# A hybrid streaming encoder on one core: another order of the mixer's streams (key rotation two steps behind the query's, projection steps between the score pairs and around the first small products)

## The chip, the cores and the metric

The kernel runs on one core of a Trainium2 chip, as one launch. The metric is the time of the whole program on the device in microseconds (us). Engines: TensorE (PE, with its weight loads PEld), VectorE (DVE), ScalarE (ACT), GpSimd (POOL) and SyncE (SP), which issues the transfers. Each engine takes its instructions in the order in which the program lists them.

## The reference

The input x is 256 rows of 1024 in float32. There are two layers, and each adds three sub-layers to x, every one between two RMSNorms: half a SwiGLU (1024 to 2816 to 1024), a token mixer, and half a second SwiGLU.

```
x += 0.5 * post1(SwiGLU_1(pre1(x)))
x += postm(W_out [GDN | DiffAttn | SSD | mLSTM](split(W_in premix(x))))
x += 0.5 * post2(SwiGLU_2(pre2(x)))
```

The mixer projects x with W_in and hands the columns to four groups of 256 columns and four heads each. A is the gated DeltaNet: a causal convolution over four rows, SiLU, l2-normalised q and k, per-head decay, and a triangular solve in chunks of 64 rows. B is differential attention: q and k rotated (rotary), two softmax maps per head, the second weighted by a scalar and taken off the first, block-causal by chunks of 64. C is an SSD (Mamba-2) with a convolution, and D an mLSTM with exponential gates and a running maximum. Their outputs, normalised, are multiplied with W_out.

## The kernel before, in words

Everything is float32, and products are made from three parts: both operands are split into a high part and the rest, and the high by high, rest by high and high by rest products are summed. The weights come from memory by SP into six raw half buffers of 128 by 1024; `split_hi` copies the high part on ACT (L177) and `split_lo` subtracts it on DVE (L328, `lo_...`). Matrix products are issued by `mm` (L203). Small helpers issue most operations, so that their lines recur: L149 `act`, L177 `acopy`, L183 `tt` and its kin, L193 and L194 `ts`, L197 `stt`.

The program is written in the order in which it is to run, with no scheduler behind it. For the feed-forward layers the order is fixed by loops. The mixer's order comes from the string `ORDER` (L40 and L41): the mixer is written as eleven Python generators, one letter each, and `interleave` (L44) takes one step of the stream that a letter names. A stream that waits for another one's result yields nothing, its letter is left in the plan, and the next letters are tried until one can step. What the blocked stream issues on its way to the wait is already in the program by then. Both layers use the same string, so each effect appears twice, 570 us apart.

The streams: `p` the projections (one step is a quarter of a 256-column projection, 12 products), `w` the weight splits, `s` the small per-head quantities (decays, their cumulative sums), `g` the gated DeltaNet, `c` the SSD, `m` the mLSTM's gates, `d` the mLSTM, `r` the attention's rotation (first the query `bq`, then the key `bk`), `x` and `y` the two pairs of attention heads, `b` the attention's end.

```
        streams = dict(s=smalls(), g=gdn(), c=ssd(), m=mlstm_gates(), r=diff(), x=diff_pair(0), y=diff_pair(1), b=diff_end(),
                       d=mlstm(), p=projections(), w=splits())
        interleave(streams, ORDER)
```

The first small products: `projections` projects the DeltaNet's keys and queries (`ps_ak`, `ps_aq`), and `ev_conv` evaluates the convolution of each, two copies with a scale on ACT (`gqk<-ps_aq`) and six multiply-adds on DVE. `smalls` makes the decay matrices (`ps_D` on PE, `eD` and `ex` exponentials on ACT, `am` on DVE); then SiLU and squares (`gqk`, `gsq`) follow on ACT, behind a table load. `mlstm_gates` begins with a transpose of `am` (`ps_am`, L889), and `gdn` with the sums of the squares (`ps_ss`, two columns) and the 64 by 64 products of keys with keys and queries (`ps_gr`). `ps_av` is the projection of the DeltaNet's values.

The attention: `diff` rotates bq and bk (a product `ps_rot`, a multiplication on DVE `rot`, one on POOL, an addition on DVE, L1392 and the lines about it). `diff_unit` has ten steps for a pair of heads, five for the second 128 rows with 256 keys (steps 1 to 5) and five for the first 128 rows with 128 keys (steps 6 to 10). Steps 1 and 2 make the scores of one map each (`ps_sc`), mask them with a memset (L1400), take the maximum (L1404, `bmx`), exponentiate on ACT (`bpe`) and take the reciprocal of the sum (L1408, `bri`). Step 3 scales and subtracts the maps on DVE, step 4 transposes the result (`ps_pT`, L1421) and copies it on ACT (`bpe<-ps_pT`), and step 5 multiplies with the values (`ps_bo`, copied by ACT to `bo`). `mlstm` makes its decay matrix (`ps_r`, then two operations `dar` on DVE and an exponential), transposes the keys `dk` (`ps_dkt`), multiplies q with k (`ps_dqk`), adds up the states (`ps_kv`, `dC`) and reads them out (`ps_di`, `ps_dq`). `lo_wo` are splits of W_out, `wo` its products. PSUM tiles come from three pools with 2, 3 and 3 buffers; `ps_sc`, `ps_pT`, `ps_bo`, `ps_dqk` and their kin share one of them.

Of the kernel before, what the change touches and what calls it, by code (L numbers as in the profile page):

```python
# [36 lines left out]
LEVELS = (1, 2, 4, 8, 16, 32)  # L37
LOG1P = (1.9999999998039973, 0.6666667925329377, 0.3999869481212616, 0.2862062340096714, 0.2139426743705339,
         0.24409403382106099)
ORDER = ("wpspwmpwpwpppsppwppswggpppgppggpwwggpwpggppwdggpgwpwcpggpcgmpggcccgggggcmgggxmxcgggxgpwwppggpggcpggw"  # L40
         "pgwgpwgwgyppwwwwwppcprgppwcwwpwywwpwdyrpxppxpyxdxxpyppxypypyppdypyxpddpbdpbdpppwppwdp")  # L41


def interleave(streams, order):  # L44

    plan = list(order)

    def step(c):
        try:
            return next(streams[c]) is not None  # L50
        except StopIteration:
            del streams[c]
            return False

    def pick():
        for n, c in enumerate(plan):
            if c in streams and c not in plan[:n] and step(c):
                return plan.pop(n)
        return next((c for c in list(streams) if step(c)), None)

    while streams:
        assert pick() or not streams, "no stream can go on"
# [59 lines left out]
def hybrid_encoder(ctx: ExitStack, tc: tile.TileContext, t_in: dict, cst_d, out_d, layers=(0, 1), stages=("f1", "mix", "f2")):  # L122
# [675 lines left out]
    def mixer(l, nxt):  # L798
# [155 lines left out]
        def splits():  # L954
            last = 2 * ids[l, "wo", WO_ORDER[3]] + 1
            for n in range(2 * ids[l, "ak"] + 2, last + 1):
                while len(parts) <= n:
                    if room.get(n, "w") == "w":
                        k = ring.index(n) - 4
                        free = k < 0 or ring[k] in used  # L960
                    else:
                        free = "ext" in ready
                    if not free:
                        yield None
                        continue
                    split_to(n)
                    yield 0.0, 1.3
# [488 lines left out]
        def mlstm():  # L1456
# [75 lines left out]
            for t in range(2):  # L1532
# [20 lines left out]
                       d=mlstm(), p=projections(), w=splits())  # L1553
        interleave(streams, ORDER)
        return accs, finish
# [63 lines left out]
```

## Time and profile before

| | |
|---|---|
| three runs | 1166.54, 1167.22, 1170.3 us; median 1167.22 |
| the profiled execution | 1166.11 us |
| its span | 1164.3 us |
| first mixer | about 205 to 403 us |
| second mixer | about 776 to 974 us |

The profile is one execution. Times of rows are microseconds from the start of its span. A row of the timeline gives the start, the busy time, the engine, the line and the operation with its output and input, and in square brackets how long the engine had been idle before and what released it. A row of the chain of waits gives the start, the length, the engine and the tile. The slices by window give for each stretch the busy time and count of each engine and at the end the clock that TensorE was granted (1.00 is full), the busy share of the transfer engines and what they moved in GB/s.

### The profile page before, as it was taken

The page shows a single profiled execution, that of the slowest core. Times are in us where ns is not written, and L with a number is a line of the kernel's source. Part 1 is how long each engine was busy: PE and PEld are TensorE (multiplying, and loading weights), DVE is VectorE, ACT ScalarE, POOL GpSimd, SP SyncE. Part 2 cuts the span into 40 slices and gives each one's busy share as a digit, 9 for nine tenths or more (in the row PEclk, how much of TensorE's full clock was granted, in tenths as well). Part 3 has the DMA queues.
Part 4 walks back from the last instruction along what each step waited for, and adds up shares of the span by engine and source line. Part 5 has one row for each costly group of instructions (what it writes and reads, how often), then busy time and mean ns, then how long its engine had stood idle before and what let it go on. Part 6 is the DMA issues. An engine that isn't in the chain of part 4 may idle for free.

```text
span 1164.3 us, 20842 instructions
## 1 busy us (share of the span) xinstructions
PE 1111.1 (95%) x8484; PEld 1031.8 (89%) x8484; DVE 742.7 (64%) x1319; ACT 569.1 (49%) x953; POOL 43.9 (4%) x64
## 2 busy tenths in 40 slices
PE   7999999899979899999999999999998898999997
PEld 5999898899968799999899999978997777999996
DVE  6745646868777865545766555477878687744552
ACT  6634545534344654543655444364434446543442
POOL 0000000010201000000000000001112010000000
PEclk9999999989989999999999999998999898999999
DMA  8856555412325466556556655634224254756630
GB/s 264 311 199 217 162 177 172 127 55 73 110 73 181 145 220 215 173 190 218 195 167 218 212 173 179 199 88 130 81 67 131 76 164 157 222 182 212 212 115 36
DMA packets 148708, 189.12 MB, mean 162 GB/s; under 512 B 12175, under 2 KB 133251, under 8 KB 148484
## 3 DMA queue, kind: packets, MB, share of 16 engines
q1 hardware_dynamic: 148612, 187.79, 50.0%
q8 instruction: 66, 1.08, 0.4%
q14 instruction: 30, 0.25, 0.1%
HBM read 186.72 MB, written 1.05 MB: 161 GB/s over the span
## 4 chain that ended last, share of the span: by engine, by line
PE 80%; DVE 11%; ACT 4%; issue 3%; POOL 1%; DMA 0%; DVEq 0%; SPq 0%; ACTq 0%; POOLq 0%
PE pgu L203 41%; PE acc L203 20%; PE wo L203 3%; PE ps_dq L203 2%; PE ps_av L203 1%; DVE gQ L183 1%; PE ps_dv L203 1%; PE ps_aq L203 1%; PE ps_ak L203 1%; PE ps_sc L203 1%; PE ps_bq L203 1%; PE ps_xT L500 1%; DVE ny L183 1%; PE ps_do L203 1%; PE ps_gr L203 1%
## 5 line engine op out<-in xcount | busy, mean ns | idle before, releaser
L149 ACT ACTIVATE sg<-pgu 128x256 f32<-128x256 f32 x88 | 33.5, 384 | 267.9 <-PE pgu L203 267.7
L203 PE MATMUL pgu<-xhi,hi_g 128*128 128x256 f32 x592 | 164.0, 277 | 0.0
L203 PE MATMUL pgu<-xhi,hi_u 128*128 128x256 f32 x592 | 163.9, 277 | 0.0
L203 PE MATMUL pgu<-xlo,hi_g 128*128 128x256 f32 x592 | 163.8, 277 | 0.0
L203 PE MATMUL pgu<-xhi,lo_g 128*128 128x256 f32 x592 | 163.6, 276 | 0.0
L203 PE MATMUL pgu<-xhi,lo_u 128*128 128x256 f32 x592 | 163.6, 276 | 0.0
L203 PE MATMUL pgu<-xlo,hi_u 128*128 128x256 f32 x592 | 163.6, 276 | 0.0
L183 DVE TENSOR_TENSOR hf<-pgu,sg 128x256 f32<-128x256 f32 x74 | 31.4, 425 | 197.4 <-ACT sg L149 197.3
L203 PE MATMUL acc<-hi_d,mlo 128*128 128x512 f32 x352 | 138.6, 394 | 0.0
L203 PE MATMUL acc<-lo_d,mhi 128*128 128x512 f32 x352 | 138.0, 392 | 0.0
L203 PE MATMUL acc<-hi_d,mhi 128*128 128x512 f32 x352 | 137.1, 389 | 0.0
L328 DVE TENSOR_TENSOR lo_g<-raw_g,hi_g 128x1024 fp32r<-128x1024 f32 x88 | 104.1, 1220 | 18.3 <-ACT hi_g L177 18.3
L328 DVE TENSOR_TENSOR lo_d<-raw_d,hi_d 128x1024 fp32r<-128x1024 f32 x88 | 103.1, 1222 | 18.3 <-ACT hi_d L177 18.3
L203 PEld LDWEIGHTS pgu<-xlo,hi_g 128*128 128x128 f32 x592 | 111.3, 188 | 1.4
L203 PEld LDWEIGHTS pgu<-xhi,hi_g 128*128 128x128 f32 x592 | 111.2, 188 | 1.3
L203 PEld LDWEIGHTS pgu<-xhi,hi_u 128*128 128x128 f32 x592 | 111.2, 188 | 0.0
L203 PEld LDWEIGHTS pgu<-xhi,lo_g 128*128 128x128 f32 x592 | 111.2, 188 | 0.0
L203 PEld LDWEIGHTS pgu<-xlo,hi_u 128*128 128x128 f32 x592 | 111.1, 188 | 0.0
L203 PEld LDWEIGHTS pgu<-xhi,lo_u 128*128 128x128 f32 x592 | 111.1, 188 | 0.0
L328 DVE TENSOR_TENSOR lo_u<-raw_u,hi_u 128x1024 fp32r<-128x1024 f32 x88 | 104.2, 1219 | 8.1 <-ACT hi_u L177 8.0
L177 ACT ACTIVATE hi_g<-raw_g 128x1024 fp32r<-128x1024 f32 x88 | 88.4, 1048 | 8.4 <-PE pgu L203 7.8
L177 ACT ACTIVATE hi_u<-raw_u 128x1024 fp32r<-128x1024 f32 x88 | 88.9, 1047 | 1.7 <-DMA raw_u<-in_ffn_w_up 0.9
(497 smaller groups left out, 2515.7 us busy)
## 6 DMA issues: line engine op xcount, KB each, us to landing
raw_g<-in_ffn_w_gate SPq DMA_DIRECT2D x88, 512.0 KB
raw_u<-in_ffn_w_up SPq DMA_DIRECT2D x88, 512.0 KB
raw_d<-in_ffn_w_down SPq DMA_DIRECT2D x88, 512.0 KB
raw_wo<-in_w_out SPq DMA_DIRECT2D x16, 512.0 KB
raw_s<-in_w_in SPq DMA_DIRECT2D x4, 528.0 KB
g_ffn_post_g<-in_ffn_post_g SPq DMA_DIRECT2D x4, 512.0 KB
raw_cz<-in_w_in SPq DMA_DIRECT2D x4, 512.0 KB
raw_ak<-in_w_in SPq DMA_DIRECT2D x4, 512.0 KB
```

The lines of the kernel that those rows point to most:

```text
L149: return nc.scalar.activation(out=out, in_=in_, func=func, **kw)
L177: return nc.scalar.activation(out=out, in_=in_, func=AF.Copy, **kw)
L183: return (eng or V).tensor_tensor(out=out, in0=a, in1=b, op=op)
L203: return nc.tensor.matmul(out, lhsT=lhsT, rhs=rhs, start=start, stop=stop)
L328: V.tensor_sub(out=lo, in0=raws[n][:, 0:w * k2], in1=hi.bitcast(F32))
L500: nc.tensor.transpose(p[:, 128 * q:128 * q + 128], self.y[:, 512 * h + 128 * q:512 * h + 128 * q + 128], ident)
```

## The change

Only the two lines of `ORDER` differ.

```
-ORDER = ("wpspwmpwpwpppsppwppswggpppgppggpwwggpwpggppwdggpgwpwcpggpcgmpggcccgggggcmgggxmxcgggxgpwwppggpggcpggw"
-         "pgwgpwgwgyppwwwwwppcprgppwcwwpwywwpwdyrpxppxpyxdxxpyppxypypyppdypyxpddpbdpbdpppwppwdp")
+ORDER = ("wpspwpwpwpppsppwspmpwgpgppgppggpwwggpwpggppwggpgwpwcpggpcgmpggcccgggggcmgggcggggpwwppggpmdggcpggwpgw"
+         "gpwgwgpppwpwcprgprpwcpwxxpyypwdxpywpxpyxdxxpypwpxypypypwpwdypwwyxxpddpbdpbdpppwppwdp")
```

In steps: the mLSTM's first step comes behind half of the projection `av`; a further quarter of `av` stands between the sums of the squares and the `gr` products; the five small gate operations of the mLSTM come later, behind copies of the DeltaNet; the key's rotation follows the query's after two projection steps, where it stood behind the mLSTM's decay matrix; the first score steps of the two head pairs stand close to each other, with projection steps between, and the mLSTM's decay matrix behind them; the last steps of the pair `x` (scaling of the first 128 rows, transposes, values) come later. The number of steps of each stream is the same, and so are the orders of POOL and SP.

On ACT, ahead of the first small products, the two scaled copies of the query change places with the exponentials of `smalls`:

```order
 L177 ACTIVATE gqk<-ps_ak,vcol 128x256 x2
 L177 ACTIVATE hi_cx<-raw_cx 128x1024
-L177 ACTIVATE gqk<-ps_aq,vcol 128x256 x2
 L149 ACTIVATE eD<-ps_D 128x512 x2
 L149 ACTIVATE ex<-cum 128x96
+L177 ACTIVATE gqk<-ps_aq,vcol 128x256 x2
 L149 ACT_TABLE_LOAD
 L149 ACTIVATE gqk<-gqk 128x512
```

The copies stand directly ahead of the table load now, with both exponentials in front of them.

On DVE, between the rotation of the query and the first scores, before:

```order
L183 TENSOR_TENSOR bq<-bq,rot 128x512
L197 SCALAR_TENSOR_TENSOR mlo<-ps_mo,vcol,mhi 128x256 x2
L328 TENSOR_TENSOR lo_dq<-raw_dq,hi_dq 128x1024
L197 SCALAR_TENSOR_TENSOR mlo<-ps_mo,vcol,mhi 128x256 x2
L328 TENSOR_TENSOR lo_dq<-raw_dq,hi_dq 128x1024
L183 TENSOR_TENSOR dar<-ps_r,am 128x512
L183 TENSOR_TENSOR dar<-dar,cst 128x512
L183 TENSOR_TENSOR rot<-ps_rot,cst 128x512
L183 TENSOR_TENSOR bk<-bk,rot 128x512
L1400 MEMSET ps_sc 64x2x64
```

And the same place in the changed kernel:

```order
L183 TENSOR_TENSOR bq<-bq,rot 128x512
L197 SCALAR_TENSOR_TENSOR mlo<-ps_mo,vcol,mhi 128x256 x2
L183 TENSOR_TENSOR rot<-ps_rot,cst 128x512
L183 TENSOR_TENSOR bk<-bk,rot 128x512
L328 TENSOR_TENSOR lo_dq<-raw_dq,hi_dq 128x1024
L197 SCALAR_TENSOR_TENSOR mlo<-ps_mo,vcol,mhi 128x256 x2
L328 TENSOR_TENSOR lo_dq<-raw_dq,hi_dq 128x1024
L1400 MEMSET ps_sc 64x2x64
```

The key's two operations moved ahead of both splits, and the two `dar` operations out of this piece: they follow now behind four score steps (memset, maximum, reciprocal, twice for each head pair), ahead of the scaling of either pair, where two score steps and their scaling alternated before.

On ACT, at the end of the attention:

```order
 L177 ACTIVATE vaug<-ps_dv 128x4x64 x2
 L177 ACTIVATE hi_wo<-raw_wo 128x1024 x2
-L177 ACTIVATE bo<-ps_bo 128x2x64 x2
+L177 ACTIVATE bo<-ps_bo 128x2x64
+L177 ACTIVATE bpe<-ps_pT 128x256
+L177 ACTIVATE bo<-ps_bo 128x2x64
 L149 ACTIVATE bor_y<-bss,lnf 128x8
 L149 ACTIVATE bor_y<-bor_y,lnf 128x8
```

One more copy of transposed probabilities stands behind the two splits of W_out here, between the last two copies of the attention's output.

More of the change, by code (lines that the diff above doesn't have):

```diff
@@ L39 @@
          0.24409403382106099)
-ORDER = ("wpspwmpwpwpppsppwppswggpppgppggpwwggpwpggppwdggpgwpwcpggpcgmpggcccgggggcmgggxmxcgggxgpwwppggpggcpggw"
-         "pgwgpwgwgyppwwwwwppcprgppwcwwpwywwpwdyrpxppxpyxdxxpyppxypypyppdypyxpddpbdpbdpppwppwdp")
+ORDER = ("wpspwpwpwpppsppwspmpwgpgppgppggpwwggpwpggppwggpgwpwcpggpcgmpggcccgggggcmgggcggggpwwppggpmdggcpggwpgw"
+         "gpwgwgpppwpwcprgprpwcpwxxpyypwdxpywpxpyxdxxpypwpwxypypypwpwdypwwyxxpddpbdpbdpppwppwdp")
 def interleave(streams, order):
```

## The prediction

> **What bounds the kernel now.** I read the page first (span, busy shares), then the waits of TensorE in the stretch of one mixer, then the stretch cut into slices of 3.41 us with the clock granted in each, and last the chain of waits and the timelines of ScalarE and VectorE at the two places that the change touches. From the page:
>
> ```profile
> PE 1111.1 (95%) x8484; PEld 1031.8 (89%) x8484; DVE 742.7 (64%) x1319; ACT 569.1 (49%) x953; POOL 43.9 (4%) x64
> ```
>
> PE is busy 95% of the span, so a change of order can give back at most the twentieth in which it stands still, and what it does more slowly than it could. The profiled execution took 1166.1 us (its span, 1164.3, and 1.8 us around it) and lies 1.1 us under the median of the three times, 1167.2. The sum below starts from 1166.1. A difference of 0.3% is 3.5 us, about the least that a measurement of this kernel tells from no change.
>
> PE's waits between 205 and 403 us, the first layer's mixer (line waited at, engine and line waited for, us in total, times, longest):
>
> ```profile
> PE ps_sc L203 <- DVE bk L183: 3.3, 1, 3.3
> PE ps_am L889 <- DVE am L183: 2.5, 1, 2.5
> PE ps_sc L203 <- ACT bpe L149: 2.3, 1, 2.3
> ```
>
> The first is the wait for the rotated keys before the first attention scores, the second the wait ahead of the first small product, the third one between two units of scores. The second layer repeats the program 570 us later, so each term counts twice. The norms, the feed-forward layers, SP's queue of transfers and POOL's queue keep their order, so those are nothing in the sum.
>
> **Term A, around the first small products.** The slices there (PE busy, PEld, DVE, ACT, POOL, then the granted clock, DMA share, GB/s):
>
> ```profile
> 232.17:235.59 3.42, 2.60 (x23) 2.63 (x24) 1.42 (x4) 3.35 (x6) 1.22 (x5) 1.00 0.16 55
> 235.59:239.00 3.41, 3.41 (x55) 3.39 (x54) 2.33 (x6) 0.44 (x1) 0.00 (x0) 0.99 0.14 26
> 239.00:242.41 3.41, 3.41 (x41) 3.29 (x38) 1.77 (x5) 0.00 (x0) 0.00 (x0) 0.50 0.40 133
> 242.41:245.83 3.42, 3.42 (x18) 3.42 (x18) 2.14 (x7) 0.00 (x0) 1.62 (x2) 0.51 0.00 0
> 245.83:249.24 3.41, 3.41 (x32) 3.41 (x32) 2.02 (x6) 0.84 (x2) 1.14 (x1) 1.00 0.00 0
> ```
>
> For two slices, 6.8 us, the clock is half, and half of that, 3.4 us, is lost. It falls right behind a slice in which PE was never idle, so idle time alone didn't do it. What PE did in that slice stands in the chain of waits (start, us, engine, tile):
>
> ```profile
> 233.26 2.75 PE ps_av L203 x24
> 236.00 1.68 PE ps_ss L203 x16
> 237.68 3.52 PE ps_gr L203 x64
> 241.21 5.11 PE ps_av L203 x24
> ```
>
> The same 24 projection products of `av` take 2.75 us before and 5.11 us behind, and between them run the sums `ss` (two columns wide) and the 64 by 64 products `gr`. My reading is that a slice full of small products counts as little work and halves the clock of the next. Now the change. The multiplication `am` goes ahead of six vector operations on DVE, and half of `av` goes ahead of `ps_am`: the wait of 2.5 us there goes. What is late next is `ss`, which needs ScalarE's squares `gsq`. ScalarE's rows (start, us, line, operation):
>
> ```profile
> 228.81 0.84 ACT L177 ACTIVATE gqk<-ps_aq,vcol 128x256 f32<-128x256 f32 x2 [0.42 <-PE ps_aq L203]
> ...
> 231.31 1.28 ACT L149 ACT_TABLE_LOAD   x1
> ...
> 234.45 0.63 ACT L149 ACTIVATE gsq<-gqk 128x512 f32<-128x512 f32 x1
> ```
>
> The copy `gqk` from `ps_aq` now stands behind the two exponentials and directly ahead of the table load, so the load starts 0.8 us later and the last `gsq` ends near 235.9 in place of 235.08. PE, which no longer waits at `am`, has half of `av` done by about 233.3 (2.75 us from 230.5, where it went idle before) and then waits 2.5 us for `gsq`: it starts `ss` at 235.9, against 236.0 before. The idle time is thus moved and not removed, which is nothing in the sum, and what is left of the term is the clock. `gr` now stands behind 12 further `av` products, 1.4 us after `ss`. The slice 232.17 to 235.59 would hold 1.1 us of PE work, the next `ss` and most of an `av` quarter, the third nearly all of `gr`. Ends: if no slice is poor enough, the 3.4 us come back (A = -3.4); with one slice at half, A = -1.7; with two again, A = 0; with three A = +1.7, and with four A = +3.4, since the first slice with its idle time could halve the clock for `ss`, `av` and `gr` alike. I take 0, the row with two slices, because `gr`, `ss` and the idle time are all still there, in the same three slices.
>
> **Term B, the score pairs and what follows.** The slices there, in the same columns:
>
> ```profile
> 331.16:334.57 3.41, 1.03 (x12) 0.78 (x12) 2.13 (x3) 0.63 (x1) 0.29 (x1) 0.99 0.48 157
> 334.57:337.99 3.42, 1.16 (x5) 0.83 (x3) 2.00 (x6) 1.02 (x4) 0.00 (x0) 0.50 0.00 0
> 337.99:341.40 3.41, 3.41 (x14) 2.75 (x13) 2.10 (x8) 1.02 (x4) 0.00 (x0) 0.50 0.00 0
> 341.40:344.81 3.41, 3.41 (x18) 3.41 (x18) 2.11 (x7) 1.02 (x4) 0.00 (x0) 0.51 0.02 5
> 344.81:348.23 3.42, 3.34 (x29) 3.15 (x29) 2.17 (x8) 3.22 (x7) 0.00 (x0) 1.00 0.00 0
> ```
>
> A slice with PE busy 1.03 of 3.41 us is followed by half clock, and two full slices pass before the clock is whole again. VectorE in the same stretch, from the timeline:
>
> ```profile
> 327.08 1.22 DVE L328 TENSOR_TENSOR lo_dq<-raw_dq,hi_dq 128x1024 fp32r<-128x1024 f32 x1
> 328.21 0.87 DVE L197 SCALAR_TENSOR_TENSOR mlo<-ps_mo,vcol,mhi 128x256 fp32r<-128x256 f32 x2
> 329.00 1.21 DVE L328 TENSOR_TENSOR lo_dq<-raw_dq,hi_dq 128x1024 fp32r<-128x1024 f32 x1
> 330.13 0.68 DVE L183 TENSOR_TENSOR dar<-ps_r,am 128x512 f32<-128x512 f32 x1
> 330.85 1.15 DVE L183 TENSOR_TENSOR dar<-dar,cst 128x512 f32<-128x512 f32 x1
> 331.92 0.68 DVE L183 TENSOR_TENSOR rot<-ps_rot,cst 128x512 f32<-128x512 f32 x1
> 332.70 0.69 DVE L183 TENSOR_TENSOR bk<-bk,rot 128x512 f32<-128x512 f32 x1
> 334.73 0.17 DVE L1400 MEMSET ps_sc<- 64x128 f32 x1 [1.34 <-PE ps_sc L203]
> ...
> 339.73 0.35 DVE L193 TENSOR_SCALAR bpe<-bpe,bri 128x256 f32<-128x256 f32 x1
> ...
> 341.40 0.17 DVE L1400 MEMSET ps_sc<- 64x128 f32 x1
> ```
>
> Each softmax unit is a chain that starts with a memset of the masked corner: a pair of them takes 5.0 us (334.73 to 339.73), and the scaling of the pair 1.7 (to 341.40). The change puts `rot` and `bk` of the key ahead of two weight splits, so that the scores are there when DVE comes to them, and moves the two `dar` operations (1.8 us) behind the chains. DVE reached the end of `bk` at 333.4; without `dar` it is through with all that stands ahead of the chains at 331.6. So the first chain starts 3.1 us earlier. But four chains now follow each other (2 x 5.0 = 10.0, to 341.6), then `dar` (1.8, to 343.4), then the scaling of the first pair (1.7, to 345.1), 3.7 us later than before. The keys are there at 333.4 less the 1.8 and less the two splits and the small `mlo` pair that now come behind them (3.3, the rows at 327.08 to 329.00), at 328.3. From then PE has two pairs of scores (1.03 us for 12 products in the slice at 331.16, 2.1 for both) and the projection `dk`, 48 products (5.5, by the 2.75 for 24 of `av`): an estimated 7.6 us, so that it is through near 336. It then stands idle for over 8 us, where it waited 5.6 in two pieces before (3.3 and 2.3). The second pair's scaling, behind one weight split (1.2, a split of `lo_dq`'s size) and 1.7 of its own, ends near 348.0.
>
> What PE does from there, in the chain of waits:
>
> ```profile
> 346.58 1.10 PE ps_bo L203 x8
> 347.68 1.44 PE ps_dq L203 x12
> ...
> 364.18 0.96 PE ps_dqk L203 x30
> ```
>
> From 347.68 to 364.18 PE ran 16.5 us without a wait, at full clock. Changed, the first `dq` product (1.44) falls ahead of the wait for the second pair, and the small product `ps_bo` (1.10) comes behind it; about 15.9 remain behind 348.1, and `ps_dqk` would start at 364.0, 0.2 us earlier than before. That is the gain of the early keys: nearly nothing, since the order of DVE, and not the keys, decides when the second pair is ready. The clock stands against it. Two whole slices (337.99 to 344.81) are idle or nearly so; the clock is half when PE resumes at 345.1, and by the rows above is whole again two slices later, at 351.64. Of 6.5 us at half clock 3.25 are lost, of which 1.0 lies in the wait that PE would have had ahead of the second pair: 2.2 net. `ps_dqk` then starts 2.0 us later than before. In the old order the slow slices cost nothing of this kind, because DVE's chains bounded that stretch.
>
> Then the tail of the attention: the last unit's transposes now wait for the scores' products on DVE (behind `lo_wo` splits), and their copy on ScalarE stands behind this row:
>
> ```profile
> 366.42 2.01 ACT L177 ACTIVATE hi_wo<-raw_wo 128x1024 fp32r<-128x1024 f32 x2
> ```
>
> The last `ps_bo` waits for that copy, and the output projection, `ps_kv` and the mLSTM's state wait behind it on PE. Bounds: nothing, if the splits come early, and 2.0, the row. I take 1.5, since splits of `wo` stand right ahead of the copy and an engine takes its queue in order. B = 2.0 + 1.5 = 3.5. Its ends are -0.2 (whole clock, tail covered) and 5.2 (one more slice at half, 1.7).
>
> A rule of the Trainium skill, the page "TensorE: Matmul & The Clock Gate", section "HAM oscillation — how this bites in real kernels", says in the abstract that there should be no idle gap of PE over about 3.4 us. By it B's gap of 8 us halves the clock, as the row at 331.16 has it; A's gap of 2.5 us would not, and the sum would be by the rule 1166.3 where it is 1173.1 by the rows. The trace speaks against it as a full account, since the clock fell at 239.00 behind a slice with no idle time.
>
> **The sum.** 2 x (0 + 3.5) = +7.0: 1166.1 + 7.0 = 1173.1 us. With B from 2.0 to 5.2 this case spans 1170.1 to 1176.5.
>
> **Rivals.** *Faster*: the clock holds at the small products (A = -3.4), because `av` pieces on both sides of `ss` and ahead of `gr` keep each slice above the fall, and the tail's copies find cover (B between -0.2 and 2.0). For it: 2.60 us of work in the slice at 232.17 didn't halve the clock, so the fall lies below that. Against it: the same slice will hold 1.1 us, close to the 1.03 that did. It gives 2 x (-3.6) to 2 x (-1.4): 1158.9 to 1163.3, the middle 1161.1. It decides where no slice between 232 and 246 is granted half.
>
> *No change*: a gain at the small products and the loss behind the pairs cancel: A = -3.4 with B = 3.5 gives 1166.3, A = -1.7 with B = 2.0 gives 1166.7. For it: `gr` leaves the slice in which `ss` runs, which is the one sure difference there. Against it: it asks for two sizes to match.
>
> *Worse than forecast*: the idle time ahead of `ss` halves the clock at once, and `ss`, `av` and `gr` all run at half: A = +1.7 to +3.4, with B = 3.5 to 5.2: 1176.5 to 1183.3. For it: 1.1 of 3.42 us busy. Against it: that slice starts and ends with wide products.
>
> That the change doesn't do what it says is excluded for the keys: on DVE `bk` moves ahead of both splits, and no other stream holds it back.
>
> **How the numbers follow.** Chances: forecast 0.38, faster 0.22, no change 0.25, worse 0.15. The time is that of the likeliest, 1173.1. For 8 in 10 the range runs from 1162 (about half of the faster case, 0.12, is left out) to 1179 (half of the worse case, 0.07). Faster by over 0.3%: 0.22. Within it: 0.25 and the lower edge of the forecast, together 0.26. Slower: the rest, 0.52.
>
> **What would show it.** Right: no wait at `ps_am`, one of about 2.5 us at `ps_ss` for ScalarE; two slices at half clock near 239 to 246; the first score memset near 331.7 and the first pair's scaling not before 345; a wait of PE of 7 us or more at `ps_pT`, half clock from before 345 to near 351; a new wait at the last `ps_bo` for ScalarE's copy. Wrong: full clock through 232 to 246 (the faster case); a wait at `ps_pT` under 4 us, or full clock behind it, which would take 2 us out of B; no wait at `ps_bo`, which takes 1.5.

## The result, and the profile after

The changed kernel takes 1177.01 us (median of 6 runs, 1173.02 to 1178.12) against 1166.88 us (median of 6, 1164.34 to 1170.3). The ratio is 1.0066, 95% interval 1.0042 to 1.0090, so it is slower by 4.9 to 10.5 us, 7.7 by the ratio itself; the medians differ by 10.1. The forecast was 1173.1.

The profiled execution of the changed kernel took 1178.1 us, near the top of its runs, and that of before 1166.1. The two traces thus differ by 12.0 us, some 2 us more than the medians do.

```profile
span 1176.3 us, 20842 instructions
## 1 busy us (share of the span) xinstructions
PE 1124.1 (96%) x8484; PEld 1040.4 (88%) x8484; DVE 742.6 (63%) x1319; ACT 569.0 (48%) x953; POOL 44.9 (4%) x64
```

The same 8484 products keep PE busy for 1124.1 us, 13.0 more than before: PE doesn't wait longer in sum, its work takes longer. Where that happens is read off marks that both traces have (the start of a tile, in us):

| start of | first mixer: before | after | later by | second mixer: before | after | later by |
|---|---|---|---|---|---|---|
| `ps_D` | 228.61 | 228.93 | 0.3 | 798.80 | 806.97 | 8.2 |
| `ps_kt` (behind the small products) | 247.50 | 251.11 | 3.6 | 817.75 | 826.07 | 8.3 |
| first `ps_sc` of the SSD | 285.43 | 289.01 | 3.6 | 855.67 | 864.85 | 9.2 |
| last `cy` (end of the SSD) | 324.28 | 328.78 | 4.5 | 894.45 | 904.65 | 10.2 |
| `ps_dqk` | 364.11 | 367.27 | 3.2 | 934.44 | 944.09 | 9.7 |
| `ps_kv` | 369.11 | 375.33 | 6.2 | 939.44 | 952.13 | 12.7 |
| first `pgu` of the next feed-forward | 401.58 | 408.88 | 7.3 | 973.35 | 985.70 | 12.4 |

Four stretches have a price: the small products 3.3 us in the first layer and 0.15 in the second; the end of the SSD 0.9 and 1.0; the score pairs a gain of 1.3 and 0.55; the tail behind `ps_dqk` 3.1 and 3.0. The rest, 2.8 of the 12.4 us, lies outside these four: 0.3 ahead of the first mark, 0.9 in the feed-forward between the mixers, 0.9 ahead of the SSD in the second layer, and behind `ps_kv` 1.1 in the first layer less 0.3 in the second. PE's waits in the first mixer, 205 to 408 us:

```profile
PE ps_ss L203 <- ACT gsq L149: 2.5, 1, 2.5
PE ps_pT L1421 <- DVE bpe L197: 1.4, 5, 0.4
PE ps_sc L203 <- DVE bk L183: 1.3, 1, 1.3
...
PE ps_bo L203 <- ACT bpe L177: 0.7, 1, 0.7
PE ps_pT L1421 <- DVE dar L183: 0.5, 1, 0.5
```

The wait for `am` is gone and one of 2.5 us for `gsq` stands in its place. The keys are waited for 1.3 us where it was 3.3. The waits for the last `ps_bo` and for `dar` are new.

**The small products, first layer.** Slices of 3.41 us; the third number from the end is the granted clock:

```profile
233.72:237.13 3.41, 0.95 (x9) 0.95 (x9) 1.76 (x7) 3.29 (x5) 0.08 (x1) 1.00 0.00 0
237.13:240.55 3.42, 3.42 (x17) 3.42 (x18) 2.51 (x6) 0.00 (x0) 0.00 (x0) 0.50 0.30 63
240.55:243.96 3.41, 3.41 (x42) 3.19 (x41) 0.00 (x0) 0.00 (x0) 0.00 (x0) 0.50 0.27 95
243.96:247.37 3.41, 3.41 (x40) 3.29 (x37) 1.59 (x4) 0.00 (x0) 0.00 (x0) 0.50 0.00 0
247.37:250.79 3.42, 3.42 (x18) 3.42 (x18) 3.00 (x10) 0.84 (x2) 1.64 (x2) 0.50 0.00 0
```

Behind the idle slice (0.95 of 3.41 us busy) the clock is half, and it stays at half for four slices, in which `ss`, `av` and `gr` all run. The chain of waits shows what that does to each:

```profile
236.18 2.74 PE ps_ss L203 x16
238.92 2.77 PE ps_av L203 x12
241.69 4.45 PE ps_gr L203 x64
```

The sums take 2.74 us where they took 1.68, 12 products of `av` take 2.77 where 24 took 2.75, and `gr` takes 4.45 where it took 3.52. In the second layer the same rows lie otherwise:

```profile
810.61:814.03 3.42, 1.13 (x10) 0.93 (x8) 2.88 (x9) 3.35 (x5) 1.19 (x5) 0.99 0.16 54
814.03:817.44 3.41, 3.22 (x15) 3.22 (x16) 1.23 (x1) 1.09 (x2) 0.00 (x0) 0.50 0.00 0
817.44:820.85 3.41, 3.41 (x17) 3.19 (x18) 1.31 (x5) 0.00 (x0) 0.00 (x0) 0.51 0.53 153
820.85:824.27 3.42, 3.42 (x73) 3.35 (x72) 1.32 (x4) 0.00 (x0) 0.00 (x0) 1.00 0.01 2
```

Here the clock is whole again at 820.85, just as `gr` starts (820.49), and as far as `ps_kt` the price is that of before, two slices. The border of a slice fell a little otherwise against the same work. But `ps_kt` follows `gr` by 5.6 us there, by 9.5 in the first layer, and PE comes up against VectorE's chain that starts with the result of `gr`:

```profile
830.50 1.13 PE L203 MATMUL ps_y<-gQ,npbd 128*128 128x128 f32 x8 [0.20 <-DVE gQ L183]
```

The second group of `ps_y` waits as long, and both are through 6.9 us behind the start of `ps_kt` where it was 6.0 in the first layer. That is the 0.9 us ahead of the SSD, so that the part costs 1.0 us in the second layer and not 0.15.

**The end of the SSD.** VectorE's rows, and then POOL's at the same time:

```profile
327.41 0.16 DVE L183 TENSOR_TENSOR crr_a<-crr_a,crr_v 128x4 f32<-128x4 f32 x1
327.61 1.07 DVE L197 SCALAR_TENSOR_TENSOR ccr<-crr_a,crr_y 128x4 f32<-128x4 f32 x1
```

```profile
327.57 1.09 POOL L183 TENSOR_TENSOR bk<-bk,cst 128x512 f32<-128x512 f32 x1 [1.42 <-PE ps_rot L203]
```

An operation on four columns takes 1.07 us in place of 0.16: it ends when POOL's multiplication of the key ends. Before, POOL came to the key at 330.35, when `ccr` was long done. It held another operation up there, the second `dar`, whose row the prediction shows with 1.15 us. With POOL idle beside it the same operation takes 0.69. POOL in the kernel before, then `dar` in the changed one:

```profile
330.35 1.10 POOL L183 TENSOR_TENSOR bk<-bk,cst 128x512 f32<-128x512 f32 x1 [7.79 <-PE ps_rot L203]
```

```profile
347.24 0.69 DVE L183 TENSOR_TENSOR dar<-dar,cst 128x512 f32<-128x512 f32 x1
```

The change thus moved a hold of 0.46 us to a place where it costs 0.91.

**The score pairs.** VectorE's first memset of the scores and the two weight splits that follow the scalings of the two pairs:

```profile
336.13 0.17 DVE L1400 MEMSET ps_sc<- 64x128 f32 x1
...
349.58 1.23 DVE L328 TENSOR_TENSOR lo_dv<-raw_dv,hi_dv 128x1024 fp32r<-128x1024 f32 x1
...
352.29 1.22 DVE L328 TENSOR_TENSOR lo_dv<-raw_dv,hi_dv 128x1024 fp32r<-128x1024 f32 x1
```

Less the 4.5 us by which the stretch starts later, these are 331.6, 345.1 and 347.8, against a forecast of 331.6, 345.1 and 348.0: VectorE did what the prediction worked out. PE's slices at the same time, first layer:

```profile
332.79:336.20 3.41, 2.66 (x12) 1.83 (x13) 3.39 (x6) 0.24 (x1) 0.00 (x0) 0.99 0.22 54
336.20:339.61 3.41, 3.41 (x15) 3.09 (x16) 1.86 (x6) 1.02 (x4) 0.00 (x0) 0.50 0.67 247
339.61:343.03 3.42, 3.42 (x16) 2.70 (x13) 1.70 (x7) 1.83 (x6) 0.00 (x0) 0.50 0.04 13
343.03:346.44 3.41, 3.41 (x12) 2.38 (x12) 1.41 (x6) 1.72 (x8) 0.00 (x0) 0.51 0.00 0
346.44:349.85 3.41, 2.84 (x24) 2.44 (x24) 3.23 (x8) 1.88 (x3) 0.00 (x0) 1.00 0.00 0
```

There is no idle stretch of 8 us. The clock fell while the scores were made, behind a slice with 2.66 us of work, PE did `dk` at half clock in the time in which it would have waited, and it was whole again before the first pair was ready. In the second layer the clock held through `dk` and PE did wait, 3.8 us in one piece, with the half clock behind it:

```profile
919.84:923.25 3.41, 0.79 (x7) 0.59 (x5) 2.16 (x6) 1.02 (x4) 0.00 (x0) 0.99 0.00 0
923.25:926.67 3.42, 2.18 (x9) 1.81 (x10) 3.26 (x7) 3.11 (x5) 0.00 (x0) 0.50 0.00 0
926.67:930.08 3.41, 3.41 (x19) 3.41 (x17) 2.37 (x4) 0.98 (x2) 0.00 (x0) 0.51 0.45 154
```

That is the course that the prediction gave for both layers, with less than half of its idle time, and the stretch gained 0.55 there against 1.3 in the first. Why PE was idle for so much less, even at full clock, stands in its rows: the scores before (first layer), and then, in the second layer of the changed kernel, the scores, `ps_r` and the transposes of the first pair:

```profile
333.54 1.19 PE L203 MATMUL ps_sc<-bk,bq 32*128 32x256 f32 x12 [3.33 <-DVE bk L183]
```

```profile
909.07 1.10 PE L203 MATMUL ps_sc<-bk,bq 32*128 32x256 f32 x4 [1.26 <-DVE bk L183]
910.50 1.13 PE L203 MATMUL ps_sc<-bk,bq 32*128 32x256 f32 x4 [0.34 <-DVE mlo L197]
...
913.13 2.25 PE L203 MATMUL ps_sc<-bk,bq 32*128 32x256 f32 x8
...
916.78 1.03 PE L203 MATMUL ps_r<-drd,cst 128*128 128x512 f32 x2
...
924.46 1.38 PE L1421 MATMUL ps_pT<-cst,bpe 128*128 128x128 f32 x4 [3.82 <-DVE bpe L197]
```

Before, 12 score products (three maps) behind one wait took 1.19 us together, though one of them lasts 0.37: they ran beside each other. In the changed kernel the four products of each map take 1.10 to 1.13, map after map, 4.5 us for all 16. With `dk`, and with `ps_r`, which moved in between, PE is through at 920.6, 11.6 us after it began.

**The tail.** Rows of PE's timeline, then the slice in which they lie and the next:

```profile
371.43 0.44 PE L1421 MATMUL ps_pT<-cst,bpe 128*128 128x128 f32 x2 [0.50 <-DVE dar L183]
372.57 0.66 PE L203 MATMUL ps_bo<-bv,bpe 128*128 128x64 f32 x4 [0.70 <-ACT bpe L177]
```

```profile
370.33:373.75 3.42, 2.22 (x14) 1.72 (x14) 3.42 (x5) 2.46 (x5) 0.00 (x0) 0.99 0.74 215
373.75:377.16 3.41, 3.41 (x38) 2.41 (x39) 0.79 (x3) 0.00 (x0) 0.40 (x1) 0.51 1.02 300
```

The transposes wait for `dar`. Their own input is ready at 368.8, but `dar` reads `ps_dqk`, which lies in the same pool of three accumulators, and stands behind two weight splits on VectorE:

```profile
370.96 0.75 DVE L183 TENSOR_TENSOR dar<-ps_dqk,dar 128x256 f32<-128x256 f32 x2
```

That the wait is one for the accumulator is read from this order; no run tested it. The last values wait for the copy behind two splits on ScalarE. The slice with both waits is 2.22 us busy, and one at half clock follows.

### The profile page after: what moved, and what is told of

Read it like the earlier page. It is cut to its first block, busy times and chain, and to the rows that moved or that the text cites. A ratio compares the mean times of both kernels' runs of the same rounds, so it can differ in the third digit from the quotient of the medians.

```text
span 1176.3 us, 20842 instructions
## 1 busy us (share of the span) xinstructions
PE 1124.1 (96%) x8484; PEld 1040.4 (88%) x8484; DVE 742.6 (63%) x1319; ACT 569.0 (48%) x953; POOL 44.9 (4%) x64
## 4 chain that ended last, share of the span: by engine, by line
PE 81%; DVE 10%; ACT 4%; issue 3%; POOL 1%; DMA 1%; DVEq 0%; SPq 0%; ACTq 0%; POOLq 0%
PE pgu L203 41%; PE acc L203 20%; PE wo L203 3%; PE ps_dq L203 2%; PE ps_bq L203 1%; PE ps_aq L203 1%; PE ps_cb L203 1%; PE ps_ak L203 1%; PE ps_xT L500 1%; PE ps_y L203 1%; DVE ny L183 1%; PE ps_dk L203 1%; PE ps_av L203 1%; PE ps_do L203 1%; PE ps_cx L203 1%
```

## The experiments

Each kernel was run against the kernel before in five rounds on the same chip. Diffs show the start of the string `ORDER` where the rest is that of the kernel before, or the piece that differs.

**The first part alone.** The small products as in the change, the attention as before.

```
-ORDER = ("wpspwmpwpwpppsppwppswggpppgppgg
+ORDER = ("wpspwpwpwpppsppwspmpwgpgppgppgg
```

> Only the change's first part (the small products); attention as before. Theory (parts): the wait for am goes and one for gsq of 2.5 us comes, and the clock decides. In the changed kernel's profile the first layer's mixer had four slices at half clock there (3.3 us later than before) and the second layer's two (0.15 us later). So this kernel costs 0 to 6.6 us more than before, by the two layers' mean 3.4 (ratio 1.003), with the wait at ps_ss in both layers. Rival (the loss sits in the attention): ratio 1.000, with two slices at half clock at this place in both layers.

Ratio 1.0027 (1.0008 to 1.0046), 3.2 us. Its profile, of an execution of 1182.1 us at the top of its runs (median 1170.84), has the wait of 2.5 us at `ps_ss` and four slices at half clock in both layers (`ps_kt` is 3.3 and 3.2 us later against `ps_D`). That execution is long for another reason too: from `cy` to `ps_dqk` the second layer took 45.5 us where it took 40.0. The theory of parts holds. The rival, that the loss sits in the attention alone, doesn't.

**The second part alone.** The small products as before, then the change's string.

```
-ORDER = ("wpspwpwpwpppsppwspmpwgpgppgppgg
+ORDER = ("wpspwmpwpwpppsppwppswggpppgppgg
```

(This diff is against the changed kernel.)

> Only the second part (early key, score pairs, tail); small products as before. Theory (parts): the tail behind ps_dqk costs 3.0 us a layer (1.4 of waits for transposes and copies, the rest one slice at half clock), the stretch from the key's rotation to ps_dqk gains 0.4 to loses 0.4: plus 5 to 7 us, ratio 1.005. Rival (the loss is the clock at the small products): ratio 1.000 to 1.001, since these are as before here.

Ratio 1.0027 (1.0014 to 1.0041), 3.2 us, below the 5 to 7 that I gave. By its marks, a layer costs 0.9 to 1.1 at the end of the SSD, gains 1.3 in the score pairs, and pays 2.3 in the tail. No slice at half clock stands behind its tail in either layer, which is the part of the changed kernel's 3.0 that is missing here. The two parts together make 1.0054, within the interval of the whole change. Its small products, in the order of before, took 1.6 us more than before from `ps_D` to `ps_kt` in the first layer, with three slices at half clock, and no more in the second: the same order isn't answered alike in every execution.

**The second part without the tail.** One step of the pair `x` back to its place (the lines are pieces of the changed string):

```
-pyxdxxpyp ... wwyxxp
+pyxdxxxpyp ... wwyxp
```

and the small products as before.

> The second part with the tail put back: the scaling, transposes and values of the pair x's first 128 rows stand where they stood before. Theory (tail): ps_kv follows ps_dqk by 5.0 us as before in place of 8.1, no half-clock slice there, and the time is that of before within 2 us (ratio 0.998 to 1.002). Rival (the pairs themselves cost, as the prediction's 2.0 us a layer had it): 4 us more than before, ratio 1.0035, with PE's half clock behind an idle stretch at ps_pT.

Ratio 1.0002 (0.9986 to 1.0017). `ps_kv` follows `ps_dqk` by 5.0 us as before. So the early key and the pairs are worth nothing in sum that this measurement could tell (1.6 us less to 2.0 more for both layers), and the 2.0 us a layer that the prediction charged them with, 4.0 in all, are refuted.

**The tail alone.** The kernel before, with the pair `x` one step late at the end:

```
-yxdxxpyp ... dypyxpdd
+yxdxpyp ... dypyxxpdd
```

> The kernel before with the change's tail alone: the scaling of pair x's first 128 rows comes behind two splits of W_out, its transposes and values behind those of pair y. Theory (the tail is a cost of its own): ps_kv follows ps_dqk by 7.3 us in place of 5.0 in both layers, 4.6 us more in all, ratio 1.004. Rival (the tail only costs because the early pairs shift what lies ahead of it): under 1 us a layer, ratio 1.001.

Ratio 1.0032 (1.0021 to 1.0042), 3.7 us or 1.9 a layer. `ps_kv` follows `ps_dqk` by 7.3 us in both layers. The waits of its profile, 360 to 380 us:

```profile
PE ps_bo L203 <- ACT bpe L177: 0.7, 1, 0.7
PE ps_pT L1421 <- DVE dar L183: 0.5, 1, 0.5
```

They are those of the changed kernel, without its score pairs: the tail is a cost of its own. Its slice with the waits, 2.29 us busy (370.02 to 373.43), wasn't followed by half clock here; in the changed kernel the one with 2.22 was.

**Three quarters of `av` ahead of `ps_am` and `ps_ss`.** The attention as before; ScalarE's order as before.

```
-ORDER = ("wpspwmpwpwpppsppwppswggpppgppgg
+ORDER = ("wpspwpwpwpppsppwpspwpmggppgppgg
```

> The attention as before; at the small products three quarters of the projection av stand ahead of ps_am and ps_ss, and the two scaled copies of the query stay ahead of the exponentials on ScalarE. Theory (idle time): PE fills the 2.5 us in which it waited for am, ss starts near 235.1 in place of 235.84 with 12 more products done, ps_kt comes 2.2 us earlier in each layer, and the half clock stays at two slices: 4.4 us less than before, ratio 0.996. Rival (the clock decides, idle time alone doesn't): the slices are as poor as before or poorer because ss and gr now follow each other, and a third slice at half clock takes 1.7 us of it back in each layer: ratio 0.999.

Ratio 0.995 (0.9933 to 0.9968), 5.8 us faster than before. PE waits 0.5 us at `ps_ss` where it waited 2.5 at `ps_am`. The clock falls for one slice in the first layer and two in the second, and again behind a slice that was busy throughout, the one with `gr` and the end of `ss`:

```profile
236.60:240.01 3.41, 3.41 (x72) 3.33 (x72) 3.10 (x10) 0.00 (x0) 0.00 (x0) 0.99 0.38 106
240.01:243.43 3.42, 3.42 (x17) 3.42 (x18) 3.28 (x10) 0.65 (x2) 0.46 (x1) 0.51 0.14 48
```

**The same with the last quarter of `av` between `ps_ss` and `ps_gr`**, as the change has a quarter there.

```
-ORDER = ("wpspwpwpwpppsppwpspwpmggppgppgg
+ORDER = ("wpspwpwpwpppsppwpspwpmgpgpgppgg
```

(Against the kernel with three quarters ahead.)

> As av ahead with the attention as before, but the last quarter of av stands between ps_ss and ps_gr, as the change has a quarter there. Theory (small products on both sides of a wide piece keep the clock down longer): one slice more at half clock in a layer on the mean, 1.7 us, so 3.4 us more than with av ahead alone, 2.4 less than before: ratio 0.998. Rival (the idle time ahead of ss was what made the change's slices poor; without it the parting is harmless): as av ahead alone, ratio 0.995.

Ratio 0.9969 (0.9955 to 0.9984). Both expectations failed in part. The clock never fell at this place, in either layer (two stretches of the first layer, `ss` and the beginning of `av` in the one, `gr` in the other):

```profile
234.90:238.30 3.40, 2.95 (x26) 2.76 (x25) 1.80 (x4) 1.54 (x2) 0.00 (x0) 1.00 0.02 5
238.30:241.70 3.40, 3.40 (x71) 3.21 (x71) 1.76 (x8) 0.84 (x2) 0.00 (x0) 1.00 0.49 154
```

So a wide piece between the small products doesn't keep the clock down: with it, and with no idle slice ahead, the clock stayed up. `ps_kt` came 4.9 us earlier against `ps_D` than before, 1.4 and 2.8 more than without the parting. But `gr` comes 1.5 us later against `ps_D` than without the parting, VectorE's work behind it too, and PE then waits:

```profile
PE ps_y L203 <- DVE gQ L183: 1.7, 2, 1.5
```

The first `ps_sc` of the SSD follows `ps_kt` by 2.2 us more than before: what the clock gave, the DeltaNet's chain on VectorE took back.

**The convolution of `av` out of VectorE's way.** The last kernel, and the one with three quarters ahead, each with the convolution moved behind the projection `cx`:

```
-            ev_conv("av", 12, gv)
-            act(flat(gv[:]), flat(gv[:]), AF.Silu)
...
                 yield from proj(nm) if nm in ("do", "bv", "dv") else proj_T(nm)
+                if nm == "cx":
+                    ev_conv("av", 12, gv)
+                    act(flat(gv[:]), flat(gv[:]), AF.Silu)
...
```

> Three quarters of av ahead of ps_am and ps_ss, the last between ps_ss and ps_gr, attention as before, and the convolution of av (six VectorE operations, 2.4 us) with its SiLUs issued behind the whole projection cx. Theory (with the clock held, VectorE's queue behind ps_gr is what took the gain back): the wait of 1.7 us at ps_y goes, the clock stays whole at the small products, ratio 0.994 or less. Rival (VectorE is full in that stretch whatever the order): the wait moves to ps_dq or ps_n, ratio 0.997 as without the move.

> The same late convolution with all of ps_gr ahead of the last quarter of av. Theory: no wait of PE stands there with av ahead, so the move is worth nothing, ratio 0.995 as without it, with half-clock slices at the small products. Rival (the late convolution by itself helps): 0.993 or less.

Ratios 1.0035 (1.0022 to 1.0048) and 1.0051 (1.0032 to 1.0070): both are slower than the kernel before, against every expectation. In the first, the wait at `ps_y` fell from 1.7 to 0.3 us as the theory had it, and the clock stayed whole at the small products in both layers. A wait that none of the theories had came (3.5 us in the second kernel):

```profile
PE ps_cb L203 <- DVE gv L197: 3.9, 1, 3.9
```

The projections take their PSUM tiles from a pool of two buffers, and `cb` waits until the convolution has read that of `av`. Behind `cx` the convolution isn't free to stand.

**The early key and pairs on top of three quarters of `av` ahead**, the tail as before.

```
-ORDER = ("wpspwpwpwpppsppwspmpwgpgppgppgg
+ORDER = ("wpspwpwpwpppsppwpspwpmggppgppgg
```

(Against the changed kernel, whose tail is put back as above.)

> Three quarters of av ahead of ps_am and ps_ss, with the change's early key and score pairs, and the tail where it stood before. Theory (the parts add up): 5.8 us from the first and nothing from the second, ratio 0.995, as with av ahead alone. Rival (the earlier small products free the keys too, so that the pairs gain more): 0.993 or less.

Ratio 0.9955 (0.9941 to 0.9969): the parts add up, and the pairs give nothing here either. The tail stands as before, and yet in the first layer a slice there with 2.71 us of work (367.39 to 370.80) was followed by half clock; in the second one with 2.71 wasn't.

**Two tests of POOL's hold**, both on that kernel: the key's `ps_rot` one projection step later, and the key's multiplication on VectorE.

```
-cprgprpwc
+cprgpprwc
```

```
-                mul(x[:], x[:], bc(K("cos"), 1, [128, 2, SEQ]), eng=G)
+                mul(x[:], x[:], bc(K("cos"), 1, [128, 2, SEQ]), eng=G if nm == "bq" else V)
```

> As the run with av ahead, early key and pairs, but the key's product ps_rot on PE stands three projection steps behind the query's instead of two, which starts POOL's multiplication of the key some 1.6 us later. Theory (POOL's multiplication holds VectorE): in the profile the small VectorE operation ccr takes 0.16 us again instead of 1.07, cy comes 0.9 us earlier, and another VectorE operation beside POOL's is longer by up to 0.9; the total is the same or up to 1.8 us less. Rival (ccr's length has another cause, the data or its operands): ccr still takes 1.07 us.

> As the run with av ahead, early key and pairs, but the key's multiplication with the cosine runs on VectorE in place of POOL. Theory (POOL's multiplication holds VectorE): ccr takes 0.16 us again, cy comes 0.9 us earlier, the multiplication costs VectorE 0.7 us ahead of the first scores: total 0 to 2 us less. Rival (VectorE's queue is what counts, whoever holds it): the 0.7 us come back ahead of the chains in each layer, the total is the same within 1 us though ccr is short.

`ccr` takes 0.16 us in both. With the key one step later, POOL's multiplication runs from 323.92 to 325.01, and another operation of VectorE is longer, 1.27 us where the same took 0.69:

```profile
324.29 1.27 DVE L183 TENSOR_TENSOR bq<-bq,rot 128x512 f32<-128x512 f32 x1
```

The hold is POOL's, then, and it moves with POOL's instruction. The ratios, 0.9962 (0.9949 to 0.9975) and 0.9959 (0.9945 to 0.9972), are the same as 0.9955. By the marks of the first layer `cy` came 0.9 and 1.1 us earlier behind the SSD, and `ps_dqk` followed it 0.6 and 1.0 us later: the gain is taken back ahead of `ps_dqk`, much as the rival of the second test had it.

The lowest ratio of these orders is that with three quarters of `av` ahead and all else as before, 0.995; the three with the early key and pairs besides can't be told from it.

## Why the prediction was right in its direction, and which steps failed

**The small products, the waits: right.** The wait for `am` went, one of 2.5 us for `gsq` came, `ss` started where it had. The idle time was moved and not removed, as the prediction said.

**The small products, the clock: mis-sized.** "I take 0, the row with two slices" failed in the first layer, where the term was 3.3, the end that the prediction gave with four slices; in the second it held as far as `ps_kt` (0.15), and VectorE's chain behind `gr`, which had no term, added 0.9. The part alone measured 3.2 us for both layers, 1.6 a layer. In the first layer this is what the rival "Worse than forecast" had as its condition: the idle time ahead of `ss` halves the clock at once, and `ss`, `av` and `gr` all run at half. The reading that slices full of small products count as little work is borne out in part. Slices with hardly anything but `ss` and `gr` were followed by half clock; those with most of `gr` and a piece of a projection weren't (238.30 to 241.70 in the parted kernel, 820.85 to 824.27 in the changed one). What the reading lacked is seen by counting the slices at half clock in each layer: with an idle slice ahead and parted small products behind it, four, two, four and four; with the idle slice alone, as in the kernel before, one to three; with neither, one or two; with parting alone, none in the four layers of two kernels. The prediction's faster rival had parting alone in mind, and lost because the change has both.

**The score pairs: VectorE right, PE wrong.** The failed step is the estimate of 7.6 us of work for PE and "it then stands idle for over 8 us". The estimate took 2.1 us for the scores, from 12 products that ran beside each other, and nothing for `ps_r`; apart, the scores take 4.5, and with `ps_r` and `dk` it was 11.6 us at full clock (second layer) and 15.4 with the clock at half for most of it (first). What was left of the wait at `ps_pT` was 3.8 us in the second layer and 1.2 in the first, in four pieces, both under the 4 us that the prediction had named as a sign of being wrong. The half clock that the prediction placed behind the idle stretch came ahead of it in the first layer, where VectorE's chains set the pace. In place of a loss of 2.0 us a layer the stretch gained 1.3 and 0.55, and with POOL's hold taken off nothing of it is left: 1.0002 without the tail.

**POOL: a term left out.** The prediction set POOL to nothing because its order is the same. Its order is, but the time of its instruction is not, and it held a four-column operation of VectorE for 0.9 us in each layer, ahead of `cy`. The row that gave a warning was among the prediction's own, `dar` with 1.15 us beside 0.69 for its like, and was taken as the operation's length.

**The tail: the mechanism right, the size too small.** 1.5 was taken, with 2.0 as its end. Alone it measured 1.9 a layer (2.3 between the marks), and in the profile of the changed kernel 3.0, with one slice at half clock behind it. The wait for `dar`, 0.5, had not been counted. The half clock behind it came in one of the two kernels with this tail and the pairs, and not in the kernel with the tail alone.

**The sum.** 7.0 was forecast and the medians differ by 10.1 (4.9 to 10.5 by the ratio). By the runs of the parts a layer has 1.6 for the small products, nothing for the pairs with POOL's hold and 1.9 for the tail, 3.5 together; the forecast had 0, 2.0 and 1.5, also 3.5. The loss by the pairs that didn't come stood in for the small products, which had been set to nothing: that the sum came out near is luck. The direction rested on the tail, the one term that was right in kind and nearly in size.

The Trainium skill, "TensorE: Matmul & The Clock Gate", section "HAM oscillation — how this bites in real kernels", speaks of idle gaps over about 3.4 us. By that rule a gap of 2.5 us would have cost no clock. The trace disagrees: the slice with this gap, 0.95 of 3.41 us busy in the first layer and 1.13 in the second, was followed by half clock in both, and so was a slice in which PE was busy throughout with `gr` and the end of `ss` (236.60 to 240.01 in the kernel with `av` ahead).

## What to carry to other kernels

An idle gap is worth filling with wide products from the same stage: that gave 5.8 us here, where a reorder that only moved the gap cost 3.2. Where small products follow a gap, look at the clock granted in the slices behind them, and put a wide piece between them only if the engine that reads their result has time to wait for it. Small products that ran beside each other before can't be priced by that row once the order sets them apart. And when a step is moved, follow the time and not the order of each instruction on each engine, and count what holds its buffers: POOL's place in the order didn't change, and the convolution that looked free held the next projection's accumulator.

## What the runs showed of the hardware that was not expected

POOL holds VectorE up. While POOL multiplied a 128 by 512 tile (1.09 us), VectorE's operation on 128 by 4 elements took 1.07 us in place of 0.16, and others on 128 by 512 took 1.27 and 1.15 in place of 0.69. All of them read two tiles from SBUF. The Trainium skill, "GPSIMD Engine Reference", section "1. Specifications", says that POOL shares its SBUF interfaces with VectorE, with contention for VectorE's instructions that have two SBUF inputs; these rows agree.

The clock's answer to the same work differs between layers of one execution: the changed kernel's small products cost four slices at half clock in the first layer and two in the second. Nor does PE's busy time in a slice settle it: 2.22 and 2.66 us (the tail and the first scores of the changed kernel) were followed by half clock, 2.29 (the tail alone) and 2.15 (906.19 to 909.60, ahead of the first scores in the second layer) weren't, and 2.71 was in one layer and not in the other. The borders of the slices lay differently against the work in most of these cases; that this is the cause was not tested.
